# One decoder layer on one core: half of the second branch's products formed inside the third attention

## The chip, the cores and the metric

The kernel runs on one core of a Trainium2 chip. The core has five engines that run side by side, each through its own list of instructions in order: PE (TensorE, the matrix engine; its weight loads have a row of their own, PEld), DVE (VectorE), ACT (ScalarE), POOL (GpSimd) and SP (SyncE, which here issues nearly all transfers between the main memory, HBM, and the on-chip memory, SBUF). Products land in PSUM, a small accumulator memory of eight banks. The metric is the device time of one execution in microseconds (us); lower is better.

## The reference, cut to what matters

The layer projects the normalised input once, runs three token mixers, multiplies each mixer's output by a matrix, weighs it with a sigmoid gate and adds the three:

```python
branches = jnp.stack([oa, ob, oc], axis=0)             # three mixers, (1024 tokens, 512) each
y = jnp.einsum('nbsm,nmd->bsnd', branches, w_branch[layer])
gate = jax.nn.sigmoid(mg.reshape(B, S, N_BRANCH, D_MODEL).astype(jnp.float32)).astype(y.dtype)
x = x + jnp.sum(gate * y, axis=2) @ w_out[layer]

h = rms_norm(x, norm_mlp[layer])
x = x + jnp.square(jax.nn.relu(h @ w_up[layer])) @ w_down[layer]
```

`oa` is a differential attention, `ob` a sliding-window attention, `oc` a sparse attention with three parts (compressed, selected, window). Everything is float32, 1024 tokens, 1024 features, mixers 512 wide.

## The kernel before, in words

Float32 products are made of three products of split operands: `split` (lines 87 to 91) copies a value to a rounded "high" part on ACT (L90) and subtracts it on DVE or POOL for the "low" part (L91); `mm3` (L118 to L120) multiplies high by high, low by high and high by low into one PSUM bank. Each 256 KB block of weights is therefore loaded (L100), copied on ACT, subtracted on POOL.

The stages in order are: norm and input projection; compressed keys; the first mixer (four heads), the second (two groups) and the third (two groups, `items_c`); then `merge_and_mlp`, which joins the branches, multiplies by `w_out` and runs the MLP.

PE's order is written by hand: PE executes what the program emits, in that order. In an attention, `mix` interleaves two generators: the attention's fine steps (logits, transposes `tr`, value products `ac`), each with an estimated PE and DVE cost, and "dense" work that depends on nothing in that attention (gate projections, branch products). Dense steps are emitted while a running count stays below a goal set by the `PACE` factor; what is left when the fine steps end is emitted after them. The other engines' orders come from a scheduler that works on estimated times.

Dense work beside the second group of the third attention (926 to 1194 us in the trace) comes from `first_branch`. A gate step (`gates`) forms one of 24 gate blocks and stores it to HBM (`gd`). For the tokens 0 to 511 and then 512 to 1023, four operand blocks of the first mixer are loaded from HBM (`od`) and split (`operand`), and for each of eight feature blocks `d` one product is made: load and split the weight `wbr`, load the gate `g` into one of two buffers (`tm`), twelve matmuls into one of two banks (`mm`), then on DVE `g = (g+1)*product` (L1162, emitted with high priority), and a store to `yd` in HBM (L1163).

The merge holds two loops. The first runs over the eight `d` and both token halves and makes the sixteen products of the second branch: gate load into one of two buffers (L1137), load of the stored `yd` block into `y` (L1195), twelve matmuls into one of six banks, DVE multiply (L1197), and on POOL the add `y = y + g` (L1199). The second makes the sixteen products of the third branch: DVE multiply (L1208) and add (L1210), then the split into `mh` on ACT (L1211) and `ml` on DVE (L1212). The eight `w_out` blocks (`wo`, 512 KB each) are loaded into two buffers `x1` (L1264) and split on POOL and DVE in turn; they are the stationary operands' partners of the `w_out` products that follow on PE. SP issues its transfers strictly in order: a transfer that waits for a buffer holds up all behind it.

## Time and profile before

| | us |
|---|---|
| median of 3 runs | 2041.63 (2040.56 to 2045.64) |
| the profiled execution | 2045.69, span 2043.7 |
| PE busy in the span | 1901.7 (93%) |
| third attention, second group, from its first dense work to its last value product | 926 to 1194 |
| merge, first loop's first product to the first `w_out` product | 1195.2 to 1290.2 |

The profiled execution is as slow as the slowest of the three runs. Busy shares in the table of stretches are what an engine did in that stretch; the column after POOL is the clock that PE was granted (1.00 is full). A row of the timeline gives the start, the duration, the engine and line, and in brackets how long the engine stood idle before it and what ended that. The span of a matmul overlaps that of the next one; the time that one costs is the distance between two starts.

### The profile page before, as it was taken

Reading aid. Unit: us, or ns where it says so; the run is one execution under the profiler, and the core shown is the slowest. Engines: PE = TensorE matmul, PEld = TensorE weight load, DVE = VectorE, ACT = ScalarE, POOL = GpSimd, SP = SyncE. Lnnn points to the kernel's source line nnn. Section 1 sums busy time; section 2 is a strip of 40 time slices with the busy share of each in tenths; the row PEclk is TensorE's granted clock in tenths of the full one; section 3 lists DMA queues with packets and bytes.
Section 4 is the critical chain, followed back from the end, with each engine's and each line's share of the span. In section 5 each row is a group of like instructions: output and inputs, shape, how many; then the busy total and the mean of one; then the engine's idle time right before and its main releaser. Section 6 shows DMA issues by size and latency. Waiting matters only on the chain. (4 is left out here: it accounts for less than half of the span.)

```text
span 2043.7 us, 30701 instructions
## 1 busy us (share of the span) xinstructions
PE 1901.7 (93%) x9838; PEld 1621.5 (79%) x9838; DVE 1423.4 (70%) x3231; ACT 1022.0 (50%) x2626; POOL 954.3 (47%) x1142
## 2 busy tenths in 40 slices
PE   7999888988799999999999899999899998999998
PEld 6888887888688888887888677787688886888876
DVE  6757777788848677648676755657755544889898
ACT  5456556666636555536555533335455544444331
POOL 4455355544352212162222227218444445789784
PEclk9999999999999999999999899999899998999999
DMA  5131022011211111212242456425444446355343
GB/s 218 51 104 52 4 55 59 26 38 37 87 28 61 56 52 51 72 33 91 68 147 77 159 198 204 147 93 161 172 167 160 144 145 247 119 167 163 124 144 114
DMA packets 122558, 219.49 MB, mean 107 GB/s; under 512 B 14420, under 2 KB 35412, under 8 KB 122396
## 3 DMA queue, kind: packets, MB, share of 16 engines
q1 hardware_dynamic: 120812, 211.75, 31.9%
q10 hardware_dynamic: 1584, 5.77, 0.9%
q8 instruction: 78, 1.28, 0.3%
q14 instruction: 84, 0.69, 0.1%
HBM read 156.59 MB, written 64.81 MB: 108 GB/s over the span
## 5 line engine op out<-in xcount | busy, mean ns | idle before, releaser
L91 POOL TENSOR_TENSOR wl<-wr,wh 128x512 fp32r<-128x512 f32 (+3 forms) x246 | 328.8, 1343 | 275.0 <-ACT wh L90 238.8
L90 ACT ACTIVATE wh<-wr 128x512 fp32r<-128x512 f32 (+3 forms) x258 | 150.3, 590 | 183.8 <-PE mm L119 124.1
L711 PE MATMUL sc<-st 128*128 128x256 f32 (+5 forms) x736 | 183.9, 344 | 25.9 <-ACT p L743 25.3
L90 ACT ACTIVATE ph<-tr 128x384 fp32r<-128x384 f32 (+3 forms) x280 | 138.4, 497 | 105.5 <-PE tr L759 87.0
L91 DVE TENSOR_TENSOR pl<-tr,ph 128x384 fp32r<-128x384 f32 (+3 forms) x280 | 155.8, 559 | 40.2 <-ACT ph L90 37.6
L756 POOL MEMSET ph<- 128x128 f32 x152 | 35.7, 235 | 291.3 <-PE ac L901 253.0
L711 PEld LDWEIGHTS sc<-st 128*128 128x128 f32 x736 | 122.8, 192 | 47.5 <-ACT p L743 38.8
L118 PE MATMUL mm<-hh,wh 128*128 128x512 f32 x384 | 158.8, 414 | 0.0
L120 PE MATMUL mm<-hh,wl 128*128 128x512 f32 x384 | 151.5, 395 | 0.0
L119 PE MATMUL mm<-hl,wh 128*128 128x512 f32 x384 | 151.4, 394 | 0.0
L119 PE MATMUL mm<-wl,wh 128*128 128x512 f32 x352 | 139.5, 396 | 9.4 <-POOL wl L91 9.4
L118 PE MATMUL mm<-wh 128*128 128x512 f32 x352 | 139.9, 398 | 8.2 <-DVE x L1471 5.3
L90 ACT ACTIVATE wh<-u 128x512 fp32r<-128x512 f32 x162 | 93.0, 620 | 106.3 <-PE mm L119 27.9
L759 PE MATMUL tr<-ident,p 128*128 128x128 f32 x792 | 129.2, 275 | 16.9 <-ACT o L889 7.8
L120 PE MATMUL mm<-wh,wl 128*128 128x512 f32 x352 | 139.1, 395 | 0.0
L743 ACT ACTIVATE p<-sc,mc 128x256 f32<-128x256 f32 (+5 forms) x200 | 106.7, 538 | 52.0 <-DVE mc L735 47.0
L901 PE MATMUL ac<-ph,st 128*128 128x256 f32 x392 | 109.8, 298 | 19.4 <-DVE ob L908 11.5
L91 POOL TENSOR_TENSOR wl<-s,wh 128x512 fp32r<-128x512 f32 x64 | 89.5, 1405 | 79.3 <-ACT wh L90 79.3
L118 PE MATMUL mm<-wh,hh 128*128 128x384 f32 (+1 forms) x320 | 117.0, 366 | 0.0
L91 DVE TENSOR_TENSOR wl<-u,wh 128x512 fp32r<-128x512 f32 x98 | 112.5, 1150 | 3.9 <-ACT wh L90 3.9
L902 PE MATMUL ac<-pl,st 128*128 128x256 f32 x392 | 106.5, 292 | 6.5 <-DVE pl L91 5.8
L91 POOL TENSOR_TENSOR wl<-u,wh 128x512 fp32r<-128x512 f32 x64 | 98.8, 1557 | 25.1 <-ACT wh L90 25.0
(311 smaller groups left out, 5771.2 us busy)
## 6 DMA issues: line engine op xcount, KB each, us to landing
ud<-u SPq DMA_DIRECT2D x112, 256.0 KB, 2.2
u<-ud SPq DMA_DIRECT2D x98, 256.0 KB, 3.3
wr<-wu SPq DMA_DIRECT2D x76, 256.0 KB, 2.8
wr<-wd SPq DMA_DIRECT2D x64, 256.0 KB, 2.9
gd<-go SPq DMA_DIRECT2D x48, 256.0 KB, 2.0
g<-gd SPq DMA_DIRECT2D x48, 256.0 KB, 3.2
wr<-wg SPq DMA_DIRECT2D x40, 256.0 KB, 2.7
wr<-wbr SPq DMA_DIRECT2D x40, 256.0 KB, 3.0
```

Source lines behind the costliest of these rows:

```text
L90: nc.scalar.activation(hi, src, AF.Copy)
L91: (eng or nc.vector).tensor_tensor(lo, src, hi.bitcast(F32), op=ALU.subtract)
L118: mm(out, lh, rh, start=first, stop=False, skip_group_check=more)
L119: mm(out, lh, rl, start=False, stop=False, skip_group_check=more)
L120: mm(out, ll, rh, start=False, stop=last, skip_group_check=more)
L711: self.nc.tensor.matmul(ps[:, off:off + k1 - k0], q[:, t * P:(t + 1) * P], k[:, k0:k1], start=i == 0, stop=i == 1)
L743: self.nc.scalar.activation(p, ps, AF.Exp, bias=m, scale=-1.0, accum_out=l)
L756: nc.gpsimd.memset(ph[0:rows, o:o + P].bitcast(F32), 0.0)
L759: nc.tensor.transpose(pt[0:rows, o:o + P], src, self.ident)
L901: nc.tensor.matmul(ac, v, ph, start=first, stop=False)
L902: nc.tensor.matmul(ac, v, pl, start=False, stop=last)
```

## The change

`first_branch` becomes `first_branches`, driven by a table `EARLY` of (branch, token half, gates before the operands, gates after them): branch 0 for both halves as before, and then branch 1 for the first half. For branch 1 a product also loads the stored `yd` block into one of two new buffers `yo`, and after the DVE multiply POOL adds it (`g = g + yo`, L1170 of the changed kernel) before the store to `yd`. The eight gate blocks of this stage are spread 1+3, 1+1 and 1+1 over the three sets instead of 1+4 and 2+1. The merge's first loop then runs for the second half alone; it still loads all sixteen `yd` blocks, splits four operands of the second mixer instead of eight, and makes eight products instead of sixteen. The branch-1 weights are loaded and split in both places.

```diff
-GATES = (2, 2, 12, 1, 4, 2)
+GATES = (2, 2, 12)
+EARLY = ((0, 0, 1, 3), (0, 1, 1, 1), (1, 0, 1, 1))
...
-    def first_branch(self):
+    def first_branches(self):
...
-        for half, n, m in ((0, GATES[3], GATES[4]), (1, GATES[5], 24 - sum(GATES))):
+        for b, half, n, m in EARLY:
...
-                self.operand(self.od[i], s, *o[i])
+                self.operand(self.od[4 * b + i], s, *o[i])
             yield from self.gates(m)
             for d in range(KT):
-                w = self.weight(self.a["wbr"][0, d], 512)
-                g = self.gate(self.sq, "tm", 2, 0, d, s)
-                ps = self.branch(0, d, [x[0] for x in o], [x[1] for x in o], w)
+                w = self.weight(self.a["wbr"][b, d], 512)
+                g = self.gate(self.sq, "tm", 2, b, d, s)
+                if b:
+                    y = self.sq.tile([P, 512], F32, name="yo", tag="yo", bufs=2)
+                    nc.sync.dma_start(y, self.yd[d, :, s])
+                ps = self.branch(b, d, [x[0] for x in o], [x[1] for x in o], w)
                 with self.tc.high_priority(offset=self.urgent):
                     nc.vector.scalar_tensor_tensor(g, g, 1.0, ps, op0=ALU.add, op1=ALU.mult)
+                if b:
+                    nc.gpsimd.tensor_tensor(g, g, y, op=ALU.add)
                 nc.sync.dma_start(self.yd[d, :, s], g)
                 yield 2.6
...
-            for s in halves:
-                for i in range(4):
-                    self.operand(self.od[4 + i], s, *[x[:, s] for x in ob[i]])
+            for i in range(4):
+                self.operand(self.od[4 + i], halves[1], *ob[i])
...
                 for half, s in enumerate(halves):
-                    g = self.gate(bg, "g", 2, 1, d, s)
                     nc.sync.dma_start(y[half][:, d], self.yd[d, :, s])
-                    ps = self.branch(1, d, [x[0][:, s] for x in ob], [x[1][:, s] for x in ob], w)
-                    nc.vector.scalar_tensor_tensor(g, g, 1.0, ps, op0=ALU.add, op1=ALU.mult)
-                    v = y[half][:, d, :]
-                    nc.gpsimd.tensor_tensor(v, v, g, op=ALU.add)
+                g = self.gate(bg, "g", 2, 1, d, s)
+                ps = self.branch(1, d, [x[0] for x in ob], [x[1] for x in ob], w)
+                nc.vector.scalar_tensor_tensor(g, g, 1.0, ps, op0=ALU.add, op1=ALU.mult)
+                v = y[1][:, d, :]
+                nc.gpsimd.tensor_tensor(v, v, g, op=ALU.add)
```

PE at the end of the third attention, before (`ac` are value products of the attention, `tr` transposes, `mm<-ob` the merge's first products):

```order
L759 MATMUL tr<-ident,p 128x128 x3
L901 MATMUL ac<-ph,st 128x256
L902 MATMUL ac<-pl,st 128x256
L901 MATMUL ac<-ph,st 128x256
L902 MATMUL ac<-pl,st 128x256
L901 MATMUL ac<-ph,st 128x256
L902 MATMUL ac<-pl,st 128x256
L901 MATMUL ac<-ph,st 128x256
L902 MATMUL ac<-pl,st 128x256
L118 MATMUL mm<-ob_14550,wh 128x512
```

The same place now (`mm<-xh` and `mm<-xl` are products of the dense work, here of the second branch):

```order
L119 MATMUL mm<-xh,wh 128x512
L120 MATMUL mm<-xl,wh 128x512
L121 MATMUL mm<-xh,wl 128x512
L902 MATMUL ac<-ph,st 128x256
L903 MATMUL ac<-pl,st 128x256
L902 MATMUL ac<-ph,st 128x256
L903 MATMUL ac<-pl,st 128x256
L119 MATMUL mm<-xh,wh 128x512
L120 MATMUL mm<-xl,wh 128x512
L121 MATMUL mm<-xh,wl 128x512
```

Before, the last seventeen transposes-and-values steps of the attention ran on PE with no dense work between them. Now the last gate block ends fourteen such steps before the end, and all eight moved products lie behind it: two together, four more one by one between the steps, and two directly behind the attention's last value products. PE's rows are the same in number, 8470.

SP in the merge, before (`wr<-od` are mixer outputs to be split, here of the third branch; `wr<-wbr` the third branch's weights; `g<-gd` gates):

```order
L1195 DMA y<-yd 128x512 x4
L1137 DMA g<-gd 128x512
L1130 DMA wr<-od 128x512 x2
L1264 DMA x_15545<-wo 128x1024
L1264 DMA x_15551<-wo 128x1024
L1267 DMA g_15522<-norm_mlp 128x1024
L1130 DMA wr<-od 128x512
L1137 DMA g<-gd 128x512 x2
L1130 DMA wr<-od 128x512 x3
L1137 DMA g<-gd 128x512
L1130 DMA wr<-od 128x512
L100 DMA wr<-wbr 128x512
```

And now, from the last `yd` blocks of the merge on:

```order
L1201 DMA y<-yd 128x512 x2
L1138 DMA g<-gd 128x512
L1131 DMA wr<-od 128x512 x2
L1138 DMA g<-gd 128x512
L1131 DMA wr<-od 128x512 x2
L1138 DMA g<-gd 128x512
L1131 DMA wr<-od 128x512
L1138 DMA g<-gd 128x512
L1131 DMA wr<-od 128x512 x3
L1138 DMA g<-gd 128x512
L101 DMA wr<-wbr 128x512 x2
L1138 DMA g<-gd 128x512
```

All eight operand loads of the third branch (before, seven; one had been issued in the attention) stand between the gates of the merge's first loop, and the third branch's first weight load stands behind the 31st gate load, which is the seventh of the eight that this loop needs. The two first `wo` loads have moved ahead of the last `yd` loads.

DVE at the end of the merge, now (`wo` are the splits of the odd `w_out` blocks; `x<-x,mm` is the first add behind a `w_out` product):

```order
L1215 SCALAR_TENSOR_TENSOR g<-g,mm 128x512
L92 TENSOR_TENSOR wo_15620<-x_15655,wo_15619 128x512 x2
L1217 TENSOR_TENSOR y<-y,g 128x512
L1215 SCALAR_TENSOR_TENSOR g<-g,mm 128x512
L1217 TENSOR_TENSOR y<-y,g 128x512
L1219 SCALAR_TENSOR_TENSOR ml<-y,mh 128x512 x2
L92 TENSOR_TENSOR wo_15624<-x_15667,wo_15623 128x512 x2
L1331 TENSOR_TENSOR x_15674<-x_15674,mm 128x512 x2
```

The split of the last `w_out` block now stands behind the last `ml`; before, it stood ahead of the last three multiplies of the third branch, and the splits of the first two odd blocks stood ahead of that branch's first multiply. SP's loads of the third to eighth `wo` block have moved to the merge's last gates as well.

More of the change, by code (lines that the diff above doesn't have):

```diff
@@ L298, in run @@
             else:
-                dense = self.first_branch()
+                dense = self.first_branches()
             self.mix(self.pipeline(self.items_c(g, st), last=True), dense, PACE[3 + g])
@@ L1179, in merge_and_mlp @@
             self.other = wx
-            ob = [[bb.tile([P, S], F32R, name=f"ob{i}{x}") for x in range(2)] for i in range(4)]
+            ob = [[bb.tile([P, 512], F32R, name=f"ob{i}{x}") for x in range(2)] for i in range(4)]
             oc = [None, None]
```

## The prediction

> **What bounds the kernel now.** I read the page's busy shares first and then the busy time by stretch around the two places that the change touches.
>
> ```profile
> PE 1901.7 (93%) x9838; PEld 1621.5 (79%) x9838; DVE 1423.4 (70%) x3231; ACT 1022.0 (50%) x2626; POOL 954.3 (47%) x1142
> ...
> core 0: us, PE busy (x) PEld busy (x) DVE busy (x) ACT busy (x) POOL busy (x), PEclk, DMA share, GB/s
> 1015.00:1060.00 45.00, 43.55 (x257) 38.19 (x256) 34.52 (x100) 26.34 (x69) 14.76 (x23) 1.00 0.56 172
> 1060.00:1116.00 56.00, 53.52 (x310) 46.43 (x309) 39.38 (x138) 32.17 (x96) 9.44 (x19) 1.00 0.17 54
> 1116.00:1168.00 52.00, 43.83 (x208) 36.37 (x207) 35.85 (x98) 26.34 (x72) 17.18 (x23) 0.87 0.56 180
> 1168.00:1194.00 26.00, 20.07 (x137) 16.84 (x136) 19.82 (x59) 15.16 (x39) 2.87 (x14) 1.00 0.12 37
> 1194.00:1201.00 7.00, 6.08 (x21) 4.74 (x20) 1.79 (x3) 1.01 (x2) 0.00 (x0) 0.76 0.59 163
> 1201.00:1255.00 54.00, 54.00 (x239) 44.62 (x239) 21.04 (x25) 16.18 (x27) 38.33 (x30) 1.00 0.78 267
> 1255.00:1268.00 13.00, 9.34 (x33) 7.02 (x32) 7.52 (x10) 2.41 (x4) 7.62 (x5) 0.87 0.63 201
> 1268.00:1290.00 22.00, 21.88 (x97) 17.81 (x97) 20.71 (x26) 9.81 (x17) 10.86 (x7) 1.00 0.48 152
> 1290.00:1302.00 12.00, 9.73 (x35) 7.21 (x34) 9.78 (x14) 5.11 (x9) 4.22 (x3) 0.86 0.79 278
> ```
>
> PE is busy 93% of the span and the change keeps every matmul, so time can only come from, or go into, PE's idle time and the time in which it runs at a lower clock. I call both "loss": the stretch minus PE's busy time, plus the stretch times (1 minus the granted clock, the column behind POOL). By row: 1.5 (1015 to 1060, where the first eight dense products lie), 2.5, 8.2+6.8 = 15.0 (1116 to 1168, the second eight), 5.9 (the attention's end without dense work), 0.9+1.7 = 2.6, none, 3.7+1.7 = 5.4, 0.1, 2.3+1.7 = 4.0. Together 37.0 us. The clock part counts some idle time twice, about 1 us.
>
> Next I asked PE's timeline what ended the long pauses.
>
> ```profile
> 1134.01 0.80 PE L711 MATMUL sc<-st 128*128 128x256 f32 x2 [2.55 <-ACT p L743]
> 1136.54 0.63 PE L119 MATMUL mm<-xl,wh 128*128 128x512 f32 x1
> 1136.96 0.63 PE L120 MATMUL mm<-xh,wl 128*128 128x512 f32 x1
> 1151.64 0.58 PE L711 MATMUL sc<-st 128*128 128x256 f32 x1 [3.20 <-ACT p L743]
> ...
> 1263.66 0.77 PE L118 MATMUL mm<-oc,wh 128*128 128x512 f32 x1 [2.99 <-DVE g L1208]
> ...
> 1282.70 0.39 PE L118 MATMUL mm<-oc,wh 128*128 128x512 f32 x1
> 1290.18 0.39 PE L118 MATMUL mm<-wo,mh 128*128 128x512 f32 x1
> 1297.97 0.79 PE L119 MATMUL mm<-wo,mh 128*128 128x512 f32 x1 [2.27 <-DVE wo L91]
> ```
>
> The pauses of 1116 to 1168 end with an exponential on ACT (L743), which had waited for DVE's maxima. The pause at 1263.66 ends with DVE freeing a bank, the one at 1297.97 with the split of a `wo` block. Behind such a pause two matmuls start 0.42 us apart (1136.54, 1136.96). At full clock 33 starts from 1282.70 to 1290.18 take 7.48 us, 0.227 us each, so a product of twelve costs 2.72 us. And a pause of 2.3 to 3.2 us thus costs its length once more or nearly: 6.8 us of clock loss for the two pauses of that stretch, 3.4 each.
>
> The Trainium skill, "TensorE: Matmul & The Clock Gate", section "What's actually happening", has the clock halved after an idle window of some 3.4 us. The halving agrees with the 0.42 against 0.227 us; the length does not, since 2.27 us were enough here, and by that rule alone no pause above would have cost more than itself. The measurement decides.
>
> Why DVE is late there:
>
> ```profile
> 1144.72 1.33 DVE L1046 TENSOR_SCALAR pc<-pc,lc 128x64 f32<-128x64 f32 x1
> 1145.98 2.98 DVE L1046 TENSOR_SCALAR p<-p,lc 128x512 f32<-128x512 f32 x2
> 1144.71 3.96 POOL L91 TENSOR_TENSOR wl<-wr,wh 128x512 fp32r<-128x512 f32 x3 [0.73 <-ACT wh L90]
> ...
> 1159.00 0.24 DVE L1046 TENSOR_SCALAR pc<-pc,lc 128x64 f32<-128x64 f32 x1
> ```
>
> While POOL ran three splits in a row (1144.71), DVE's scaling of a 64-wide tile took 1.33 us against 0.24, and two 512-wide ones 2.98. Eight operand splits of the second mixer fall into the same stretch:
>
> ```profile
> L91 DVE TENSOR_TENSOR ob<-wr,ob 128x512 fp32r<-128x512 f32 x8 | 6.0, 754 | 3.9 <-ACT ob L90 3.9
> ```
>
> **The change part by part.** The rows for its operations:
>
> ```profile
> L90 ACT ACTIVATE wh<-wr 128x512 fp32r<-128x512 f32 (+3 forms) x258 | 150.3, 590 | 183.8 <-PE mm L119 124.1
> ...
> L91 POOL TENSOR_TENSOR wl<-wr,wh 128x512 fp32r<-128x512 f32 x35 | 46.8, 1339 | 80.8 <-ACT wh L90 78.0 <-DVE lc L1044 2.7
> ...
> L1162 DVE SCALAR_TENSOR_TENSOR g<-g,mm x16: 677/686/689, 1018.3 to 1166.9; 128x512 f32<-128x512 f32 x16
> ...
> L1199 POOL TENSOR_TENSOR y<-y,g x16: 1281/1293/1847, 1202.3 to 1256.3; 128x512 f32<-128x512 f32 x16
> ...
> wr<-wbr SPq DMA_DIRECT2D x12, 256.0 KB, 3.2
> yd<-g SPq DMA_DIRECT2D x8, 256.0 KB, 2.2
> g<-gd SPq DMA_DIRECT2D x8, 256.0 KB, 3.2
> ```
>
> *Added outright:* eight weight blocks of branch 1 are loaded and split a second time: 8 x 0.59 = 4.7 us on ACT, 8 x 1.34 = 10.7 us on POOL. The eight adds are moved on POOL, 8 x 1.29 = 10.3 us, and the eight multiplies on DVE, 8 x 0.69 = 5.5 us. Transfers added: eight weights, eight `yo` loads, eight more stores, 24 x 256 KB = 6.3 MB. Where they land, POOL is busy 2.9 us of 26 and the transfer share is 0.12 (1168 to 1194), so as busy time they are covered. I charge nothing; without that cover the dearest of them, POOL's 21.0 us, would lie on the path.
>
> *Removed:* eight products, 21.8 us, from the merge; the same 21.8 us come to PE in the attention (16.3 before its last value products, 5.4 behind them). Net zero on PE; the sum is over losses.
>
> *Second set of branch 0.* It now runs without the operand splits of the second mixer, which cannot start before the last gate block frees their memory. Bounds: 1.5 as the first set, 15.0 as now. It is the first set's kind of work: 2.
>
> *The moved set and the attention's end.* All eight products lie in the last fourteen transposes-and-values steps, where PE now loses 5.9 us because each step waits for ACT and DVE; dense work fills such waits. Against that, four of the eight `ob` splits stay beside it (0.75 each on DVE), and a gate buffer is held longer: load 3.2, multiply 0.69, then the new add 1.29 and the store 2.2, 7.4 us for one of two buffers, 3.7 us a product against 2.72 on PE. Two products stand together and the third 3 us behind them, so DVE can wait for a gate there, with the maxima and `pl` splits queued behind it, and PE's two banks are then full. SP's later gates and weights stand behind a store that waits for POOL. Bounds: 0 and 15.0, the stretch that has the same ingredients and twice the splits. I take one pause with its clock loss, 3.2+3.4 = 6.6, and 2.4 of short ones: 9.
>
> *Attention to merge.* Now 2.6; two dense products cover the last steps. Bounds 0 and 2.6; I take 1.
>
> *Inside the merge.* The rows:
>
> ```profile
> 1195.24 0.71 PE L118 MATMUL mm<-ob,wh 128*128 128x512 f32 x1 [0.92 <-DVE ob L908]
> ...
> 1202.27 1.29 POOL L1199 TENSOR_TENSOR y<-y,g 128x512 f32<-128x512 f32 x1 [9.84 <-DMA y<-yd]
> 1256.34 1.72 POOL L1199 TENSOR_TENSOR y<-y,g 128x512 f32<-128x512 f32 x1
> ...
> 1272.96 1.27 DVE L1208 SCALAR_TENSOR_TENSOR g<-g,mm 128x512 f32<-128x512 f32 x2
> 1277.87 1.37 DVE L1208 SCALAR_TENSOR_TENSOR g<-g,mm 128x512 f32<-128x512 f32 x2
> 1304.02 1.34 DVE L1208 SCALAR_TENSOR_TENSOR g<-g,mm 128x512 f32<-128x512 f32 x2 [2.30 <-DMA g<-gd]
> ...
> 1288.27 0.86 SPq L1264 DMA_DIRECT2D x<-wo  x2
> ```
>
> Sixteen POOL adds took from 1202.27 to 1256.34, 3.60 us each against 2.72 on PE, because a gate buffer comes free only with the add. Before, PE's lead over that chain cost 5.4 us at 1255 to 1268. With eight adds it has half the length. But the third branch's first weight load now stands behind a gate load that waits for the fifth add. The first add comes 7.0 us after the first product (1195.24 to 1202.27), the fifth 4 x 3.60 later, at 21.4; then load 3.2, copy 0.59, POOL 1.34: 26.6 us, against 21.8 us for PE's eight products. A wait of 4.8 with 1.7 of clock. The `yd` loads start beside the two products before the merge's first, which may bring the first add nearer. Bounds: 0, and 12 if DVE is held three times more by a late gate as at 1304.02 (4.8 + 3 x 2.30); I take 6 for the 5.4.
>
> *`w_out` blocks.* The last two loads were issued at 1288.27, 1.9 us before the first `w_out` product (1290.18), and PE waited 2.27 us for the last split at 1297.97. Now they stand behind the last gate load. If the third branch's multiplies keep pace, they do so with two per 4.9 us (1272.96 to 1277.87, against 5.44 on PE), and the last blocks come about as late as now: 4.0. Bounds: 0, and 15 if DVE ends as far behind PE as at 1304.02, 13.8 us.
>
> *Sum.* 1.5 + 2.5 + 2 + 9 + 1 + 6 + 0.1 + 4 = 26.1 against 37.0, a gain of 10.9. The profiled execution took 2045.69 us (span 2043.7), so it would take 2034.8; it lies 4.1 above the median, 2041.63, so the median would be 2030.7. **I predict 2031 us.** With all low bounds (5.6 in all) the median would be 2010, with all high (63.7) 2068.
>
> **The rivals.**
>
> *Everything fills.* The moved set pauses no more than the first set, 1.5, and the merge starts branch 3 without a wait: losses of 15, median 2020. For it speaks the 1015 to 1060 row, which has gates and weights in the same flow; against it the longer gate chain.
>
> *The merge gives it back.* PE reaches branch 3 with its weights and operands unloaded (12 instead of 6) and the `wo` blocks come 6 us later (10 instead of 4): losses of 38, median 2043, no change. For it speak SP's order and the 2.30 us that a late gate cost DVE at 1304.02; against it the lead of the two dense products ahead of the merge.
>
> *Slower: POOL beside the attention's DVE.* Sixteen more POOL instructions of 1.3 us fall where DVE's scalings feed PE. A meeting costs DVE 1.1 us and more (0.24 to 1.33), and if PE runs dry, 3.2+3.4 = 6.6 us. One is in my sum; with two more the gain is gone (10.9 - 13.2), from the third on it is slower by over 6 us: 26.1+19.8 = 45.9, median 2051. Against it: POOL would be busy 24 of 42 us there (2.9+21.0 in 26+16.3), so meetings are likely, but one of 1.1 us counts only where PE has nothing else queued, and the dense work gives it something. The Trainium skill, "SBUF — State Buffer", section "Who interferes with whom", states this as a rule, a lock that the loser waits for in full; the 1.33 against 0.24 us agrees, and it speaks against the change.
>
> That the move does not take place can be left out: PE's order shows it.
>
> **How the numbers follow.** Chances: forecast 0.47, everything fills 0.13, given back 0.26, slower 0.14. A measurement of this kernel tells some 0.3% from no change, 6.1 us, so faster means below 2035.5. The forecast's own range is 2024 to 2037; a tenth of it is not faster. Faster 0.13 + 0.43 = 0.56; within 0.24 of the 0.26 and 0.04 of the forecast, 0.28; slower 0.14 and the 0.02 that is left, 0.16. The range reaches to the given-back case and into the slower one: 2018 to 2047.
>
> **What would show it.** Right: the stretch with the second eight products at full clock with under 3 us of loss; under 10 us of loss from the last gate block to the merge; a wait of 3 to 6 us before the third branch's first product, ended by a weight split. Wrong: half clock twice or more in the attention's last 50 us, with DVE scalings of over 1 us beside POOL adds; DVE waiting for gates there; or more than 8 us lost ahead of the `w_out` products.

## The result: 2064 us against 2041, slower

The changed kernel took 2064.02 us (median of 4 runs, 2059.5 to 2067.6), the kernel before beside it 2041.10 (2039.7 to 2045.6): a ratio of 1.0105, with a 95% interval from 1.0084 to 1.0126. That is 22.9 us slower; I had forecast 10.6 us faster, and 2064 lies outside my range. The profiled execution took 2062.41 us, with PE busy for 1897.9 us (1901.7 before). No product was added. The loss is again idle time and clock.

To compare the traces I start at one instruction, a product for the attention's logits (`sc`) behind a pause of 1.10 us. It starts at 949.27 before and at 943.15 after; this lead of 6.1 us arises ahead of the place of the change. (Over the profiled executions of the table below the start lies between 939.2 and 952.0 us, so a good part of the spread between executions arises ahead of it.) The stretches by time, before: three fixed lengths of the attention, the rest up to the merge's first product, the second branch's products, the third branch's, and the first 22.27 us of `w_out` products.

```profile
949.27:1019.27 70.00, 67.50 (x386) 58.86 (x387) 49.18 (x159) 40.10 (x114) 13.63 (x29) 1.00 0.19 60
1019.27:1064.27 45.00, 42.77 (x257) 37.55 (x256) 35.47 (x105) 26.00 (x71) 12.94 (x22) 1.00 0.55 169
1064.27:1184.27 120.00, 105.43 (x574) 89.72 (x573) 85.94 (x272) 66.61 (x186) 28.43 (x50) 0.94 0.32 103
1184.27:1195.24 10.97, 8.83 (x60) 7.15 (x58) 6.32 (x12) 5.01 (x10) 1.05 (x6) 1.00 0.19 56
1195.24:1240.48 45.24, 45.24 (x192) 37.28 (x193) 15.98 (x21) 9.48 (x15) 23.81 (x19) 0.96 0.82 277
1240.48:1290.18 49.70, 45.91 (x193) 36.94 (x192) 34.85 (x42) 19.54 (x34) 32.99 (x23) 0.97 0.57 182
1290.18:1312.45 22.27, 20.00 (x80) 15.72 (x79) 16.14 (x25) 7.49 (x13) 4.78 (x4) 0.92 0.54 192
```

The same stretches after the change (columns as in the prediction: length, then busy time of PE, PEld, DVE, ACT and POOL, the granted clock, the transfer share, GB/s):

```profile
943.15:1013.15 70.00, 65.33 (x374) 56.79 (x375) 49.53 (x151) 37.58 (x106) 15.96 (x30) 1.00 0.31 97
1013.15:1058.15 45.00, 39.92 (x229) 34.76 (x228) 32.73 (x97) 24.63 (x68) 9.23 (x17) 0.92 0.34 107
1058.15:1178.15 120.00, 111.77 (x625) 95.80 (x624) 89.27 (x275) 68.41 (x189) 33.07 (x52) 1.00 0.38 119
1178.15:1218.34 40.19, 26.64 (x143) 22.22 (x143) 17.29 (x31) 11.13 (x26) 13.64 (x20) 0.93 0.58 186
1218.34:1251.04 32.70, 24.26 (x97) 19.15 (x97) 12.99 (x15) 8.57 (x15) 16.36 (x13) 0.87 0.84 290
1251.04:1297.73 46.69, 46.50 (x192) 37.79 (x193) 37.66 (x40) 21.13 (x37) 30.97 (x23) 0.94 0.64 202
1297.73:1320.00 22.27, 15.06 (x40) 9.07 (x39) 14.14 (x19) 6.90 (x12) 8.78 (x6) 0.69 0.59 183
```

| stage, profiled | before | after | difference, without the 21.8 us that moved |
|---|---|---|---|
| to the merge's first product (rows 1 to 4) | 246.0 | 275.2 | +7.4 |
| second branch (16 products; now 8) | 45.2 | 32.7 | +9.2 |
| third branch (16 products) | 49.7 | 46.7 | -3.0 |
| first `w_out` product to the span's end | 753.5 | 762.8 | +9.3 |

Together 22.9 us, as in the medians. The losses (idle plus missing clock, as in the prediction, so that idle time at a lower clock is counted partly twice) show the pattern in the first stage. Rows 1 and 2 lost 4.7 us and now lose 13.3; row 3 lost 21.8 and now loses 8.2; row 4 lost 2.1 and now loses 16.4. The filling that I forecast took place in row 3. It was lost again ahead of it and behind it.

What ended the long pauses on PE after the change:

```profile
1037.63 0.80 PE L712 MATMUL sc<-st 128*128 128x256 f32 x2 [4.37 <-ACT p L744]
1188.92 0.58 PE L903 MATMUL ac<-pl,st 128*128 128x256 f32 x1 [3.70 <-DVE pl L92]
1218.34 0.80 PE L119 MATMUL mm<-ob,wh 128*128 128x512 f32 x1 [7.06 <-ACT wh L91]
1251.04 0.79 PE L119 MATMUL mm<-oc,wh 128*128 128x512 f32 x1 [8.30 <-ACT wh L91]
1303.06 0.50 PE L119 MATMUL mm<-wo,mh 128*128 128x512 f32 x1 [2.44 <-ACT wo L91]
1310.75 0.80 PE L119 MATMUL mm<-wo,mh 128*128 128x512 f32 x1 [2.05 <-ACT wo L91]
```

And what these releasers had waited for:

```profile
1031.05 0.63 ACT L91 ACTIVATE xh<-wr 128x512 fp32r<-128x512 f32 x1 [1.71 <-DMA wr<-od]
1033.52 0.63 ACT L91 ACTIVATE xh<-wr 128x512 fp32r<-128x512 f32 x1 [1.46 <-DMA wr<-od]
1036.28 0.63 ACT L91 ACTIVATE wh<-wr 128x512 fp32r<-128x512 f32 x1 [1.45 <-DMA wr<-wg]
...
1215.59 0.69 DVE L1168 SCALAR_TENSOR_TENSOR g<-g,mm 128x512 f32<-128x512 f32 x1 [6.30 <-DMA g<-gd]
1216.36 1.26 POOL L1170 TENSOR_TENSOR g<-g,yo 128x512 f32<-128x512 f32 x1 [5.71 <-DMA y<-yd]
1217.65 1.67 ACT L91 ACTIVATE wh<-wr 128x512 fp32r<-128x512 f32 x3 [11.42 <-DMA y<-yd]
...
1247.57 0.93 SPq L101 DMA_DIRECT2D wr<-wbr  x2
...
1283.28 2.18 ACT L91 ACTIVATE wo<-x 128x512 fp32r<-128x512 f32 x4
```

The pause at 1037.63 belongs to the second operand set of the first branch: its splits, and that of a gate block's weight, stand in ACT's order ahead of the attention's exponentials and wait there for their loads. The pause at 1188.92 ends with a low part (`pl`) of the attention's weights, split on DVE. The merge's first weights were split at 1217.65, the moment that the last of the moved adds on POOL ended (1216.36 and 1.26). The third branch's first weight was issued at 1247.57, as predicted behind gate and operand loads. The first `w_out` split came at 1283.28, 32 us after the third branch's first product; before, it came 0.6 us after that product:

```profile
1241.04 2.18 ACT L90 ACTIVATE wo<-x 128x512 fp32r<-128x512 f32 x4
```

Two of these may be matters of address, which the built programs tell. The second `yo` tile lies at bytes 103,008 to 105,056 of a partition, the merge's first split weight at 103,904 to 105,952, so the two overlap. And the pool of the second branch's operands shrank from 32 to 16 KB, since it holds one half. So the first two `w_out` blocks, at 178,144 to 194,528 as before, now lie over the third branch's operands for the first half instead of the second branch's, and must wait for them.

### The profile page after: what moved, and what is told of

Read it like the earlier page. It is cut to its first block, busy times and chain, and to the rows that moved or that the text cites. A ratio compares the mean times of both kernels' runs of the same rounds, so it can differ in the third digit from the quotient of the medians.

```text
span 2060.5 us, 30779 instructions
## 1 busy us (share of the span) xinstructions
PE 1897.9 (92%) x9838; PEld 1615.1 (78%) x9838; DVE 1435.8 (70%) x3231; ACT 1027.6 (50%) x2634; POOL 964.7 (47%) x1150
## 3 DMA queue, kind: packets, MB, share of 16 engines
q1 hardware_dynamic: 124268, 218.04, 32.7%
## 5 line engine op out<-in xcount | busy, mean ns | idle before, releaser
L92 POOL TENSOR_TENSOR wl<-wr,wh 128x512 fp32r<-128x512 f32 (+3 forms) x254 | 339.3, 1343 | 273.9 <-ACT wh L91 223.4
L91 ACT ACTIVATE wh<-wr 128x512 fp32r<-128x512 f32 (+3 forms) x266 | 155.1, 591 | 190.9 <-PE mm L120 98.5
L760 PEld LDWEIGHTS tr<-ident,p 128*128 128x128 f32 x792 | 93.3, 142 | 21.9 <-ACT o L890 10.4
```

What stands on the lines that cost most here:

```text
L91: nc.scalar.activation(hi, src, AF.Copy)
L92: (eng or nc.vector).tensor_tensor(lo, src, hi.bitcast(F32), op=ALU.subtract)
L760: nc.tensor.transpose(pt[0:rows, o:o + P], src, self.ident)
```

## The experiments

Medians, each beside the kernel before on the same chip, which stood at 2040.1 to 2042.8 us. Stages are counted in each kernel's own profiled execution from the same `sc` product as above; one execution stands for each kernel there, so a difference of a few us between two rows is not shown. Every edit also lets the scheduler choose new orders for the engines other than PE, and what that alone does was not measured.

| kernel | median (us), interval of the ratio | to the merge | 2nd branch | 3rd branch | `w_out` to end |
|---|---|---|---|---|---|
| after | 2064.0, 1.0084 to 1.0126 | 275.2 | 32.7 | 46.7 | 762.8 |
| e1 yo in the gate's tile | 2062.8, 1.0069 to 1.0126 | 273.1 | 28.0 | 46.8 | 765.6 |
| e2 pool padded | 2053.6, 1.0034 to 1.0077 | 275.4 | 31.6 | 48.7 | 749.9 |
| e3 old gate places | 2065.0, 1.0082 to 1.0135 | 269.0 | 35.5 | 48.5 | 763.5 |
| e4 no sum | 2059.6, 1.0052 to 1.0107 | 271.1 | 30.2 | 46.9 | 763.4 |
| e5 both repairs | 2058.3, 1.0066 to 1.0128 | 273.8 | 27.7 | 53.6 | 757.1 |
| e6 third gate tile | 2067.1, 1.0099 to 1.0173 | 267.2 | 27.9 | 57.0 | 769.7 |
| e7 three merge gates | 2075.2, 1.0142 to 1.0204 | 276.9 | 29.7 | 55.2 | 767.7 |
| e10 halves swapped | 2063.1, 1.0080 to 1.0124 | 273.9 | 23.5 | 54.8 | 763.2 |
| e11 three raw tiles | 2062.3, 1.0071 to 1.0120 | 275.5 | 27.8 | 53.5 | 754.5 |
| e12 gate pairs | 2047.5, 1.0014 to 1.0049 | 274.4 | 27.2 | 53.4 | 750.4 |
| e13 all three | 2063.0, 1.0062 to 1.0124 | 268.9 | 23.9 | 57.5 | 763.7 |
| e14 one weight | 2050.2, 1.0024 to 1.0052 | 270.0 | 26.6 | 54.0 | 748.6 |
| e15 pairs, old gates | 2050.0, 1.0023 to 1.0063 | 274.1 | 27.4 | 55.0 | 755.7 |
| e17 bare products, before | 2052.7, 1.0037 to 1.0071 | 258.8 | 43.7 | 51.7 | 751.6 |
| e19 inputs kept | 2051.6, 1.0043 to 1.0079 | 273.5 | 26.5 | 53.7 | 751.8 |

The three kernels with another pace (e9, e16, e18) have another order ahead of that product and are not in the table.

### The addresses

e1 loads `yo` into the unused half of the gate's tile:

```diff
-                g = self.gate(self.sq, "tm", 2, b, d, s)
                 if b:
-                    y = self.sq.tile([P, 512], F32, name="yo", tag="yo", bufs=2)
+                    gy = self.sq.tile([P, 2, 512], F32, name="gy", tag="tm", bufs=2)
+                    g, y = gy[:, 0, :], gy[:, 1, :]
+                    nc.sync.dma_start(g, self.gd[b * KT + d, :, s])
                     nc.sync.dma_start(y, self.yd[d, :, s])
+                else:
+                    g = self.gate(self.sq, "tm", 2, b, d, s)
```

> The changed kernel, with the first branch's value (yo) loaded into the unused second half of the gate's tile instead of into two tiles of its own, so that the attention's pool is no larger than in the kernel before. In the changed kernel one of the two yo tiles lies at the addresses of the merge's first split weight. Theory (addresses): the merge's weights are loaded and split before the attention ends, as they were before, and the pause of 7.06 us on the first merge product (released by the split wh on ScalarE) goes, with some 3 us of half clock behind it; the weights being ahead, the third branch's first weight (8.30 us) also comes earlier in part. Time 2048 to 2058 us against 2064. Rival (DMA traffic): the y loads of the merge fill the DMA from 1208 us on whatever the addresses, the pause stays under another name (ob or gate loads), time 2060 to 2067 us.

The merge's weights were then split in time, and another wait stood in the place:

```profile
1212.48 0.69 DVE L1171 SCALAR_TENSOR_TENSOR gy<-gy,mm 128x512 f32<-128x512 f32 x1 [5.96 <-DMA gy<-gd]
1213.32 0.77 PE L119 MATMUL mm<-ob,wh 128*128 128x512 f32 x1 [5.40 <-DVE gy L1171]
```

The second branch became 4.7 us shorter in the profile, but the median, 2062.8, is that of the changed kernel within the interval: the forecast of 2048 to 2058 failed, and the rival was right that the pause stays under another name. The weights had been late, and so had the last moved product's gate. The rival's cause, transfers that fill the DMA, does not suffice: more room for the gates took the pause away (e6 and e12 below).

e2 keeps the pool at its old size:

```diff
+            bb.tile([P, 4096], F32, name="gap2")
             ob = [[bb.tile([P, 512], F32R, name=f"ob{i}{x}") for x in range(2)] for i in range(4)]
```

> The changed kernel, with the merge's pool bb kept at its old 32 KB by an unused 16 KB tile. In the changed kernel that pool shrank to 16 KB, since the second branch's operands are of one half only, and so the first two w_out blocks lie over the third branch's operands instead of the second's. Theory (addresses): the w_out splits wait in the changed kernel until the third branch's first half is over; with the old size they start after the second branch, the w_out loads are issued some 30 us earlier and the pauses of 7.2 us idle and 5.7 us of clock between 1298 and 1316 us shrink to the 4 of the kernel before. The other two waits stay. Time 2053 to 2058 us. Rival (queue order or DMA traffic makes the w_out blocks late): 2060 to 2067 us.

2053.6 us, within the 2053 to 2058 of the theory. The first `w_out` split came 2.0 us after the third branch's first product (1256.64), and the `w_out` products ran without a pause (the stretch, then the split on ACT):

```profile
1305.36:1327.63 22.27, 22.27 (x102) 18.48 (x101) 15.71 (x23) 6.69 (x12) 5.75 (x4) 1.00 0.50 177
```

```profile
1258.66 2.18 ACT L91 ACTIVATE wo<-x 128x512 fp32r<-128x512 f32 x4
```

An unused tile of 16 KB gave back 10 of the 23 us. e5 has both:

> The changed kernel with both address repairs: yo in the second half of the gate's tile, and the pool bb padded to its old 32 KB. Theory: the two add. The padding alone took the median from 2064.0 to 2053.6 us, the yo tiles' repair alone took 4 us in the profiled run's own stretches; together 2046 to 2051 us, the first w_out product without the pauses after it, and the first merge product still behind a pause of some 5 us that the multiply on the gate of the last moved product releases. Rival: the repair of the first wait shifts the w_out loads back into the weights' way and the padding is worth less: 2052 to 2058 us.

2058.3 us: they do not add; that is the upper end of the rival's figures. The `w_out` loads now went out at 1246.50, 1249.43 and 1256.98, from the third branch's very start (1246.36) on, where the weights of that branch stand, and the third branch took 53.6 us instead of 48.7. That the one makes the other is not shown: in the kernel before two of them went out at 1247.33, 6.9 us into that branch, and it took 49.7.

### The gate's tile

The next three kernels build on e5. The edit of e6, shown against e5:

> Both address repairs, and a third tile for gate and yo of the moved products (every third product takes it; the merge's weights are pushed 1152 bytes further so that they lie over none of the three). Theory (turnover of the gate's tile): a moved product needs its tile for the gate's load, the multiply, GpSimd's addition and the store, some 8 us for two tiles against 5.4 us of TensorE for two products, and that is why the first merge product waited 5.40 us for the multiply on gy; with three tiles the pause falls under 2 us: 2040 to 2046 us. Rival (the gate loads wait behind the y loads and w_out loads on the queue, not for a tile): the pause stays at 4 to 6 us and the time is that of both repairs within 3 us.

```diff
-    gy = self.sq.tile([P, 2, 512], F32, name="gy", tag="tm", bufs=2)
+    gy = self.sq.tile([P, 2, 512], F32, name="gy", **(dict(tag="tg", bufs=1) if d % 3 == 2 else dict(tag="tm", bufs=2)))
...
+            bg.tile([P, 288], F32, name="gap3")
```

> Both address repairs, and three tiles instead of two for the merge's gates. Theory (order of the queue at the third branch's start): the weight for the third branch's first products stands behind gate loads that wait for a free tile; a third tile lets them pass, and the pause before the first third-branch products (8.30 us in the changed kernel, 3.15 and 1.54 us with yo in the gate's tile) falls under 2 us: 3 to 6 us less than both repairs alone. Rival (it waits for the operand loads and their splits, or for a weight buffer): the pause stays, the time is that of both repairs within 3 us.

```diff
-                g = self.gate(bg, "g", 2, 1, d, s)
+                g = self.gate(bg, "g", 3, 1, d, s)
...
-                    g = self.gate(bg, "g", 2, 2, d, s)
+                    g = self.gate(bg, "g", 3, 2, d, s)
```

e9 is e6 with another pace:

> The kernel with three gate tiles and both address repairs, and the pace of the dense work in the third attention raised from 1.45 to 1.5, by which all eight moved products stand inside the attention's order and none behind it. Theory A (the attention has no more room: its pauses are waits on ScalarE and VectorE that products do not shorten): the attention's last product comes some 5 us later, the merge begins at the same time, and the time is that of the kernel with three tiles within 3 us. Theory B (the room is there, and the two products left behind were the ones that would have filled it): the attention ends at most 2 us later and the time is 3 to 6 us less than with three tiles.

```diff
-PACE = (1.6, 1.4144, 1.156, 1.392, 1.45, 1.7)
+PACE = (1.6, 1.4144, 1.156, 1.392, 1.5, 1.7)
```

All three were spoilt by a side effect that I had not seen: they push the merge's split weights past byte 116,192, into the pool in which the `w_out` blocks are loaded. In the built programs they overlap there with the tile of the MLP's norm gains (116,192 to 120,288), not with those of the `w_out` blocks; why these are then loaded late too is not shown. In e6, PE and the transfers that SP issues:

```profile
1211.42 0.47 PE L119 MATMUL mm<-ob,wh 128*128 128x512 f32 x1 [0.87 <-DVE gy L1171]
...
1291.44 0.90 SPq L1276 DMA_DIRECT2D x<-wo  x2
1299.30 15.39 SPq L1276 DMA_DIRECT2D x<-wo  x6
```

No `w_out` load left before 1291.44, and the medians (2067.1, 2075.2, 2071.4 us) measure that as much as anything. What can be read: with a third tile the pause before the merge's first product fell from 4.67 us (e5) to 0.87, so the turn of the gate's tile had made it. A third gate in the merge did not shorten the third branch's first wait (5.40 us in e7, 3.25 in e5), which speaks against that theory as far as a spoilt run can.

e12 makes the same room without new memory: two gates share one tile, and `yo` takes the tiles of the gate outputs. The pool is padded as in e2.

```diff
-                    y = self.sq.tile([P, 512], F32, name="yo", tag="yo", bufs=2)
+                    if d % 2 == 0:
+                        gy = self.sq.tile([P, 2, 512], F32, name="gy", tag="tm", bufs=2)
+                    g = gy[:, d % 2, :]
+                    nc.sync.dma_start(g, self.gd[b * KT + d, :, s])
+                    y = self.rp.tile([P, 512], F32, name="yo", tag="raw", bufs=2)
...
+            bb.tile([P, 4096], F32, name="gap2")
```

> Both address repairs in another form: the gates of two moved products share one tile of the attention's pool, so that four can be in flight, and yo takes the tiles that the gates' outputs used; the pool is no larger than in the kernel before, and the merge's weights lie where they did. The third gate tile's kernel and the one with three merge gates had pushed the merge's weights over the tiles of the w_out loads, which were then issued only at 1291 and 1301 us. Theory (turnover): without that side effect the pause before the first merge product (4.67 us with two tiles) falls under 1.5 us and nothing else changes: 4 to 6 us less than both repairs, 2052 to 2055 us. Rival: the time won there is lost at the third branch's first weight: 2056 to 2060 us.

2047.5 us over ten runs, better than forecast. The pause before the merge's first product is 0.87 us, and the `w_out` products run as in e2:

```profile
1301.54:1323.81 22.27, 22.27 (x99) 18.10 (x98) 16.15 (x22) 5.96 (x11) 5.08 (x4) 1.00 0.46 145
```

So e12's two repairs together took 16.5 us off the median: 10.4 by the padding (e2) and 6.1 more by the tiles of the gates and of `yo` (the intervals of e2 and e12 overlap). These were waits for memory, tiles over others that were still in use and too few tiles in turn; which part of the 6.1 us belongs to which is not shown. The rest, 0.1 to 0.5% over the kernel before, no variant removed. By stages (e12 against the kernel before, the moved 21.8 us taken out) 6.6 us of it lie in the attention, 3.8 in the second branch and 3.7 in the third, with 3.1 gained from the first `w_out` product on; that is 11.0 us in the profiled executions, against 5.3 in the medians. The stage up to the merge stayed as long as it was: the pause at its end went, but those at the second operand set and at the `pl` split grew, from 4.37 and 3.70 to 5.47 and 5.84 us.

### The merge's cover

e10, on e5, takes the second half first through the third branch and loads the first half's `y` and operands during those eight products:

```diff
-            for half, pool in ((0, br), (1, bl)):
+            for half, pool in ((1, br), (0, bl)):
...
-                for half, s in enumerate(halves):
-                    nc.sync.dma_start(y[half][:, d], self.yd[d, :, s])
+                s = halves[1]
+                nc.sync.dma_start(y[1][:, d], self.yd[d, :, s])
...
-            for half, s in enumerate(halves):
-                for i in range(4):
-                    self.operand(self.od[8 + i], s, *oc[half][i])
-            for half, s in enumerate(halves):
+            for i in range(4):
+                self.operand(self.od[8 + i], halves[1], *oc[1][i])
+            for half, s in ((1, halves[1]), (0, halves[0])):
                 for d in range(KT):
                     w = self.weight(a["wbr"][2, d], 512)
+                    if half:
+                        nc.sync.dma_start(y[0][:, d], self.yd[d, :, halves[0]])
+                        if d % 2:
+                            self.operand(self.od[8 + d // 2], halves[0], *oc[0][d // 2])
```

> Both address repairs (2058.3 us), and in the merge the second half of the tokens goes first through the third branch; the first half's stored values y and third-branch operands are loaded during those eight products and no longer during the second branch's eight. Theory A (the moved products were the cover of the merge's loads: 4 MB of y and the operands now have 22 us of products to hide behind instead of 44): with half of them deferred, the 10 us that the third branch loses between its first product and the first w_out product (53.6 us for 43.5 us of products) and the 5 us pause at its start shrink by 5 to 10 us together: 2048 to 2054 us. Theory B (VectorE, busy 9.6 to 9.8 of 10 us in the third branch, sets its length): nothing changes there, 2055 to 2061 us.

2063.1 us; both theories are wrong on the time. The second branch took 23.5 us for its 21.8 of products, the shortest of all, so those loads had stood in its way there (27.7 us in e5). But the first `w_out` products need the first half, now the last to be finished, and waited for it:

```profile
1308.79 0.80 PE L119 MATMUL mm<-wo,mh 128*128 128x512 f32 x1 [3.72 <-ACT mh L1225]
```

> Gate pairs, three raw tiles, halves swapped, and the padded pool together. If the three causes (splits behind operand loads in the attention, turnover of the gate's tile behind it, loads without cover in the merge) are separate and each is worth what its theory says, 2036 to 2046 us, level with the kernel before (2041.5). If the loss only moves from wait to wait, because VectorE, GpSimd, ScalarE and the DMA together have as much work in the merge as before and TensorE 22 us less, it stays at 2050 to 2060 us.

2063.0 us, outside both ranges. e13 has 23.9 us in the second branch and the same new wait at `w_out`, so it does not decide between its two theories.

### The attention

e3 and e15 put the gates of the third branch back to their old places, in the changed kernel and in e12:

```diff
-EARLY = ((0, 0, 1, 3), (0, 1, 1, 1), (1, 0, 1, 1))
+EARLY = ((0, 0, 1, 4), (0, 1, 2, 1), (1, 0, 0, 0))
```

> The changed kernel, with the third branch's gates left where the kernel before has them (1, 4, 2, 1) and the moved set with no gate before or inside it. Theory: the 4.37 us pause at 1037 us comes from the second set's operand loads, whose splits stand in ScalarE's order ahead of the attention's exponentials, and from where the gates put them; with the old order the stretch up to the moved set loses what it lost before (about 6 us to 1116 us), and the moved set fills what is left of the attention's end: attention's loss 25 to about 18, time 2054 to 2062 us. Rival (the moved products only take the place of work that would have filled the same pauses): attention's loss stays within 3 us of 25, time 2061 to 2068 us.

> The kernel with gate pairs and the padded pool (2047.5 us), with the third branch's gates at the places that the kernel before has (1, 4, 2, 1) and none with the moved set. Theory A (the pause of 4 to 5.5 us at the second operand set comes from that set standing one gate earlier, and nothing else changes): 3 to 6 us less, 2041 to 2045 us. Theory B (as with the same gates on the changed kernel itself, 2065 against 2064 us, the pauses come back where the moved set loads): within 3 us of 2047.5.

2065.0 and 2050.0 us, no gain in either. In e3 rows 1 and 2 lose 5.2 us again instead of 13.3, with no pause at the second operand set, but row 3 loses 20.2:

```profile
941.23:1011.23 70.00, 67.50 (x386) 58.88 (x387) 49.22 (x159) 40.10 (x114) 13.68 (x29) 1.00 0.19 60
1011.23:1056.23 45.00, 42.28 (x255) 37.10 (x254) 34.79 (x103) 25.46 (x70) 13.04 (x22) 1.00 0.58 180
1056.23:1176.23 120.00, 107.05 (x578) 91.34 (x577) 83.23 (x254) 64.60 (x178) 31.77 (x49) 0.94 0.39 123
```

What that row holds is shown by ACT and PE:

```profile
1151.26 0.63 ACT L91 ACTIVATE xh<-wr 128x512 fp32r<-128x512 f32 x1 [0.77 <-PE mm L121]
...
1160.80 0.80 PE L119 MATMUL mm<-xh,wh 128*128 128x512 f32 x1 [4.95 <-ACT wh L91]
```

The moved set's first product waits, with no gate block in front of it. There are operand tiles for one set, so a set's splits can only begin as the last one's products end (the first split, at 1151.26, was released by such a product), and gate blocks are what PE does meanwhile. Eight gate blocks covered two sets; now they have to cover three. I take it that in both places tried one set is short of them; a kernel with more cover was not run.

e4 leaves out the sum inside the attention, with its loads and additions:

```diff
-                    y = self.sq.tile([P, 512], F32, name="yo", tag="yo", bufs=2)
-                    nc.sync.dma_start(y, self.yd[d, :, s])
...
-                    nc.gpsimd.tensor_tensor(g, g, y, op=ALU.add)
```

> The changed kernel without the sum inside the attention: the products of the second branch's first half are stored without the first branch's value, so the yo loads, their tiles and the eight GpSimd additions are left out (the output lacks that term). Theory: GpSimd's additions cost the attention nothing; what goes is the pause that the yo tiles' addresses make, so the time is that of the kernel with yo in the gate's tile within 3 us (2048 to 2058 us). Rival (GpSimd beside VectorE in the attention, or the longer chain from product to stored value, slows it): the attention itself is 5 to 10 us shorter than in that kernel, and the time 2040 to 2048 us.

2059.6 us, neither figure: too slow for both. The stage up to the merge took 271.1 us, 4.1 less than in the changed kernel. Of the 25.1 us over the kernel before, 21.8 are the moved products; against the same products without any side work (e17 below, 258.8 us) 12.3 of 16.4 us stay. So the additions with their loads are not the main cause. They do cost DVE something where they meet. After the change, ahead of the pause at 1188.92:

```profile
1028.16 0.16 DVE L1043 TENSOR_TENSOR lc<-lc 128x2 f32<-128x2 f32 x1 [0.17 <-ACT p L744]
...
1181.74 0.69 DVE L1168 SCALAR_TENSOR_TENSOR g<-g,mm 128x512 f32<-128x512 f32 x1 [1.18 <-DMA g<-gd]
1182.81 1.00 DVE L1043 TENSOR_TENSOR lc<-lc 128x2 f32<-128x2 f32 x1
1184.06 1.09 DVE L1045 TENSOR_TENSOR lc<-lc,cgate 128x3 f32<-128x3 f32 x1
...
1182.51 1.29 POOL L1170 TENSOR_TENSOR g<-g,yo 128x512 f32<-128x512 f32 x1 [0.62 <-DVE g L1168]
1183.86 2.49 POOL L92 TENSOR_TENSOR wl<-wr,wh 128x512 fp32r<-128x512 f32 x2
```

The same two-element operation took 0.16 us with POOL idle (1028.16) and 1.00 us while POOL added (1182.81). The Trainium skill, "SBUF — State Buffer", section "Who interferes with whom", describes it as a lock that the loser waits for in full; these rows agree.

e11, on e5, gives the loads of the attention three raw tiles (where weights and operands land before their split) instead of two:

```diff
-WRC = 2
+WRC = 3
```

> Both address repairs (2058.3 us), and three raw tiles instead of two for the weights and operands that are loaded during the third attention. Theory A (the attention's pauses come from splits that stand in ScalarE's order and wait there for an operand load which two raw tiles let out late; 1.71, 1.46 and 1.45 us in a row before the pause of 4.37 us in the changed kernel): the pause at 1039 us falls under 2 us and those at 1181 and 1192 us shrink too: attention 4 to 9 us shorter, 2049 to 2055 us. Theory B (the pauses have other releasers as near): the pause moves on, attention within 3 us, 2055 to 2061 us.

2062.3 us, no gain: the pause at the second set fell from 4.33 to 2.98 us, with a new one of 1.16 ahead of it, and the stage took 275.5 us.

e16 puts all eight moved products inside the attention (the pace as in e9, on e12), and e14 uses one split weight for all eight:

> The kernel with gate pairs and the padded pool (2047.5 us), with the pace of the dense work raised from 1.45 to 1.5, so that all eight moved products stand inside the attention. Theory A (no room in the attention): last attention product 4 to 6 us later, time within 3 us of 2047.5. Theory B (the two products left behind would have filled pauses at the end, and their operands' tiles come free earlier for the merge): 2040 to 2044 us.

> The kernel with gate pairs and the padded pool (2047.5 us), with one split weight used for all eight moved products: seven weight loads, seven splits on ScalarE and seven on GpSimd are left out of the attention's end (so the moved half of the second branch is computed with a wrong weight). Theory A (the side work of the moved products, not their matmuls, makes the new pauses in the attention: the pl pause of 5.84 us and the sc pauses): the attention, 268 us from the first sc pause to its last product, becomes 5 to 10 us shorter, 2038 to 2043 us. Theory B (the pauses are the chains of the attention's own rows, which products in TensorE's order cannot shorten): the attention stays within 3 us, 2044 to 2050 us.

```diff
-                w = self.weight(self.a["wbr"][b, d], 512)
+                if not (b and d):
+                    w = self.weight(self.a["wbr"][b, d], 512)
```

2048.6 us (1.0009 to 1.0044) and 2050.2 us, as e12 within the spread: where the last two products stand and the seven weights do not decide. e14's profiled execution (2041.96 us, the fastest of its five) has an attention 4.4 us shorter than e12's; the median does not bear it out.

e17 and e18 ask whether there is room at all. They are the kernel before, with eight products more that nobody reads:

```diff
+            if half:
+                for d in range(KT):
+                    self.branch(0, d, [x[0] for x in o], [x[1] for x in o], w)
+                    yield 2.6
```

> The kernel before, with eight more products behind the first branch's second set in the attention's dense work: the same operands and the last weight once more, 96 matmuls whose results nobody reads, with no load, split, multiply, addition or store of their own. Their TensorE time is 8 times 2.72 = 21.8 us. Theory A (the third attention has no idle time that products can fill; its pauses are chains in TensorE's own order): the first merge product comes 20 to 24 us later than in the kernel before, time 2060 to 2066 us. Theory B (the forecast: about 10 us of idle time at the attention's end is there to be filled, and in the changed kernel the side work of the moved products ate it): the first merge product comes 9 to 14 us later, time 2050 to 2056 us.

> The same eight bare products in the kernel before, with the pace of the dense work raised from 1.45 to 1.5, so that all eight stand inside the attention and none behind it. Theory A (no room): the first merge product 20 to 24 us later than before, 2060 to 2066 us. Theory B (room that the two products left behind would fill): 9 to 14 us later, and less than with the old pace; 2048 to 2056 us.

2052.7 and 2048.8 us (1.0021 to 1.0055), 10.8 and 6.9 us over the kernel before, for 21.8 us of products. In e17's profile the merge's first product came 12.9 us later than before, as theory B had it, and the attention lost less than ever:

```profile
939.16:1009.16 70.00, 67.50 (x386) 58.91 (x387) 49.19 (x159) 40.14 (x114) 13.64 (x29) 1.00 0.19 59
1009.16:1054.16 45.00, 42.72 (x257) 37.50 (x256) 35.30 (x105) 25.90 (x71) 13.05 (x22) 1.00 0.53 169
1054.16:1174.16 120.00, 109.14 (x597) 93.53 (x596) 84.25 (x263) 64.40 (x180) 27.70 (x48) 0.97 0.33 103
1174.16:1197.98 23.82, 22.65 (x132) 18.99 (x131) 9.89 (x21) 7.86 (x17) 1.41 (x8) 1.00 0.20 56
```

Losses of 2.5, 2.3, 14.5 and 1.2, together 20.4 us against 28.6 in the kernel before. So the room of some 10 us that I had forecast is there, for bare matmuls; it holds about half of the 21.8 us.

e19 looks for what takes it: e12 without the inputs of the moved products.

```diff
-            o = [self.parts(tag="x") for _ in range(4)]
-            for i in range(4):
-                self.operand(self.od[4 * b + i], s, *o[i])
+            if not b:
+                o = [self.parts(tag="x") for _ in range(4)]
+                for i in range(4):
+                    self.operand(self.od[i], s, *o[i])
...
+                if not (b and d):
+                    w = self.weight(self.a["wbr"][b, d], 512)
```

> The kernel with gate pairs and the padded pool (2047.5 us), with the input side of the moved products left out: no operand set of their own (the first branch's second set is used again) and one split weight for all eight; their matmuls, gates, yo loads, multiplies, additions and stores stay (the moved half of the second branch is computed from wrong operands). Measured so far from the first sc pause to the first merge product: 246.0 us in the kernel before, 258.8 with eight bare products, 274.4 with gate pairs, 270.0 with one weight. Theory A (the inputs: four operand loads and splits in ScalarE's order, and the turn of the operand tiles between the sets): 258 to 264 us, time 2036 to 2042 us. Theory B (the output side: gate and yo loads, the multiply on VectorE, GpSimd's addition, the stores): 268 us or more, time 2045 to 2051 us. Between them: both.

2051.6 us and 273.5 us to the merge, theory B's side: against e12 (274.4) the inputs are not what takes the room. Against e17, 15.5 us of loss are left (35.9 against 20.4): 8.5 in rows 1 and 2, where the new gate places put the second operand set, and the rest at the end, where this kernel still has gate loads, multiplies, additions and stores. Which of these it is stays open. So does what the new gate places cost alone, since no kernel had the old places and no third operand set together with real results.

## Why the prediction was wrong, step by step

*Rows taken over unchanged (1.5 + 2.5).* The first step that failed. I priced the first set and what follows it as before, though the diff takes one gate block from behind the first operand set and one from ahead of the second. With the new places rows 1 and 2 lost 13.3 us and more in the changed kernel, e12, e14 and e19; with the old ones 4.7 to 5.2 in the kernel before, e3, e15 and e17.

*Second set of branch 0 (2) and moved set with the attention's end (9).* Mechanism right, in part: row 3 went from 21.8 to 8.2 us with the clock at 1.00, as a fall from 15.0 to 2 would have it (8.8), and from 1166 to 1206 two pauses of 1.79 and 3.70 us, with the clock and shorter ones, came to 8.7 us, where I had 9. DVE did wait for a gate (1.18 us at 1181.74) with the small operations behind it beside POOL, as I had written.

*Attention to merge (1, bounds 0 to 2.6).* The step that failed worst. I took the old loss as the upper bound of a place that the change rebuilds. It lost 7.06 us idle, and 3.4 of clock with the products behind the pause (17 us at 0.80 from 1206), 10.5 us where I had 1. I had worked out that a gate's tile is held for 7.4 us and that two are too few, and applied it inside the attention only. I had not asked at which addresses the new tiles lie.

*Inside the merge (6, bounds 0 to 12).* The mechanism came as described: the third branch's first weight behind gate loads, ended by a weight split. Its size was 8.30 us of pause against 4.8, and 13.4 us with the clock (14.3 us at 0.64 from 1242.74): above the upper bound. What I had too small was the chain of the adds:

```profile
1227.58 1.30 POOL L1206 TENSOR_TENSOR y<-y,g 128x512 f32<-128x512 f32 x1 [5.47 <-DVE g L1204]
1243.24 1.26 POOL L1206 TENSOR_TENSOR y<-y,g 128x512 f32<-128x512 f32 x1 [2.21 <-DVE g L1204]
...
1245.45 0.42 SPq L1138 DMA_DIRECT2D g<-gd  x1
```

The first add came 9.2 us after the first product (1218.34), where I had 7.0; the fifth, at 1243.24, came 24.9 us after it, where I had 21.4. The gate load that waited for it left at 1245.45 and the weight load behind that at 1247.57.

*`w_out` blocks (4, bounds 0 to 15).* 14.1 us, near the upper bound, by another mechanism. I reckoned with DVE's lag behind PE. It was the pool that shrank, and with the old size (e2) that loss was gone. The order that I quoted showed the loads moved to the merge's end; I read it as a matter of the queue and did not ask what held them.

*The rivals.* "The merge gives it back" had the right places and too small a price: it had 38 us in all. "POOL beside the attention's DVE" had the right sign; its meetings are there, but without the additions (e4) 12.3 of the 16.4 us that the stage has over bare products were still there. None had an address in it.

## What to carry to other kernels

A change that adds a tile to a pool, or makes a pool smaller, moves what later lies on those bytes: ask of each later tile what it now has to wait for, above all where the change's own diff has only a width in it. Price moved filler work by its whole chain (operand tiles, gate tile, the queues in order), not by its matmuls: about half of the bare ones fitted here, and of the real ones hardly any. And a stage from which products are taken keeps its loads, which those products had covered (23.5 us in e10 against 27.7 in e5).

## What had not been expected

Eight bare products of 21.8 us put off the merge by 12.9 us in the profile, and cost 10.8 and 6.9 us in two medians. Eight real ones put it off by 21.3 us (e6) to 30.9 us (e7), and by 24 us or more where their weights, their operands or their additions were left out.

Executions of one program spread by some 10 us: ten of e12 lay between 2040.9 and 2054.0 us, four of the changed kernel between 2059.5 and 2067.6, thirteen of the kernel before, beside e14, between 2036.8 and 2048.1. A single profiled execution can be 8 us off its median (e14) or 10 (e15), and where a profile and a median disagreed (e1, e14) I went by the median.
